# Mixture of experts: tokens gathered for two experts at a time, and the branch for crowded experts ahead of them

## The chip, the core and the metric

The kernel runs on one core of one Trainium2 chip. The metric is the device time of one execution in microseconds (us). PE is the matmul engine, ACT, DVE and POOL are the scalar, vector and general engines, SP issues the transfers.

## The reference

Four layers over 256 tokens of width 1024: two of a first kind (attention, feed-forward, a gated side input) and two of a second kind. Layer 1 of the first kind has a mixture of experts in place of its feed-forward, and there the change lies:

```python
def moe_swiglu(x, w_router, w_gate, w_up, w_down):      # x: 256 x 1024
    logits = (x @ w_router).astype(jnp.float32)         # 8 experts
    top_v, top_i = lax.top_k(logits, TOP_K)             # TOP_K = 2
    top_w = jax.nn.softmax(top_v, axis=-1)
    gates = jnp.sum(jax.nn.one_hot(top_i, N_EXPERTS) * top_w[..., None], axis=-2)
    out = jnp.zeros_like(x)
    for e in range(N_EXPERTS):                          # w_gate[e], w_up[e]: 1024 x 3584, w_down[e]: 3584 x 1024
        out = out + gates[..., e:e + 1] * swiglu(x, w_gate[e], w_up[e], w_down[e])
    return out
```

All is float32. The weights of the eight experts are 352 MB, which is 672 tiles of 128 x 1024 (512 KB each), 84 for each expert. The 256 tokens make 512 places with the experts, 64 for each on average.

## The kernel before

Nothing is issued where it is written. The builder's calls are recorded by `Plan` as operations; a list scheduler (`order`, `choose`, run in several passes over modelled costs, `simulate` and `backwards`) then writes out one order for each engine, and all recorded operations are issued from line L755 (copies on ACT from L753). Transfers all go through SP's queue, in the planned order, and cost what `RATE` (bytes per us) says. `keep_fast` puts dummy matmuls (bf16 `identb`, 128 x 512) into stretches where the model sees PE idle, to keep its clock up. Tiles of on-chip memory are slots of tags (mx 15, raw 5, w4 8, v4 4, kv 2); a transfer into a slot can start when the slot's last reader is done. In the expert stage `raw_moe` gives the order in which weight tiles take tags: a string of 30 places.

The stage (`moe`): `route` turns the router's logits into ranks, the place of every token with its expert (`pos`), the counts per expert (`count`), the largest of them (`most`) and the gates (`gg`). Then for each expert: `gather_whole` makes one-hot matrices of `pos` and multiplies the tokens `xs` (a high and a low part, fp32r) by them, 32 matmuls of 128 columns for up to 128 places. The hidden width 3584 goes in four chunks (1024, 1024, 1024, 512). For each, `expert_up` does gate and up, `expert_out` the chunk's part of down; that makes twelve calls of `tiled` per expert. Weights are the moving side of these matmuls and tokens the stationary side: for the first 64 places each tile takes two matmuls of 64 x 512 (`x2` in an order, four records in a trace). Behind that come two guarded blocks, one if the expert has over 64 tokens and one if over 96, each with 32 places and four matmuls of 32 x 256 per tile. A guarded block is a real branch on PE against a register with the expert's count (the registers are read on L750, the branches are L732). Products of gate and up are transposed on PE (28 blocks per expert), and `combine` scatters an expert's output back to the tokens with its one-hots.

In the middle of expert 4, behind its first chunk, stands `overflow_experts`: a branch of all engines on `most` (read on L1617, branch and its end on L294). If an expert has over 128 tokens, a loop goes through all weights for the tokens beyond 128. On this input it is jumped over. At this branch an engine has finished what stands ahead of it, and SP waits until its transfers have landed.

The guarded blocks, as they are recorded:

```python
for q in range(2):
    with nc.group((count, 64 + 32 * q, 0.5 - 0.5 * q)):   # the last number: share of the cost that the planner takes
```

Of the kernel before, what the change touches and what calls it, by code (L numbers as in the profile page):

```python
# [130 lines left out]
class Op:  # L131
    __slots__ = ("idx", "engines", "calls", "cost", "preds", "succs", "need", "tiles", "cp", "end", "eng", "done",
                 "table", "bytes", "start", "seq", "pri", "late", "after", "port", "columns", "when")
# [100 lines left out]
class Plan:  # L234
# [61 lines left out]
    def add(self, engines, method, args, kw):  # L296
# [13 lines left out]
        if engines == (DMA,):  # L310
            v = out if isinstance(out, View) else args[1]
            op.bytes += v.arr.size * SIZE[v.dtype]
        for e in op.cost:
# [58 lines left out]
    def paths(self, ops):  # L372

        for op in reversed(ops):
# [4 lines left out]
            op.cp += min(op.cost.values()) if e != DMA else 1.1 + op.bytes / self.RATE  # L379

    def order(self, ops, state, aside):
# [72 lines left out]
        out = []  # L454
        for _ in range(len(ops)):
# [17 lines left out]
            if e == DMA:  # L473
                op.start = max(op.start, state["dma"] - 6.0)
                go = max(state["dma"], op.start + 1.1)
                state["dma"] = op.end = go + op.bytes / self.RATE
# [181 lines left out]
    def backwards(self, segments, orders):  # L658
# [17 lines left out]
        for op in sorted(flat, key=lambda o: -o.end):  # L676
# [6 lines left out]
            if op.eng == DMA:  # L683
                run = op.bytes / self.RATE
# [55 lines left out]
    RATE = 370e3  # L740
# [42 lines left out]
class Net:  # L783
    def __init__(self, ctx, tc, a, out):
# [4 lines left out]
        self.raw_moe = ([("mx", 15), ("raw", RAW), ("mx", 15), ("w4", 8)] * RAW  # L789
                        + [("mx", 15), ("v4", 4), ("mx", 15), ("kv", 2)] * 2 + [("mx", 15), ("w4", 8)])  # L790
# [565 lines left out]
    def route(self, lg):  # L1356

        nc = self.nc
        rank = self.sm([128, 2, 8], "rank")
# [29 lines left out]
        nc.vector.tensor_copy(self.count, pt)  # L1389
        s1 = self.sm([128, 2, 8], "s1")  # L1390
# [18 lines left out]
        gg = self.one([128, 2, 8, 2], "gg", F32R)  # L1409
        nc.vector.tensor_copy(gg[:, :, :, 0], s1)  # L1410
        nc.vector.tensor_tensor(out=gg[:, :, :, 1], in0=s1, in1=gg[:, :, :, 0].bitcast(F32), op=OP.subtract)
        return gg, pos
# [7 lines left out]
    def gather_whole(self, e, xs, pos):  # L1420

        nc = self.nc
        P = self.one_hots(e, pos)
        xg = self.t4([128, KT, 128], "xe")
        for k0 in (0, 4):
            ps = self.pc([128, 4, 128], "gth")
            with nc.group():
                for k in range(4):
# [3 lines left out]
            self.copy_out(xg[:, k0:k0 + 4], ps)  # L1432
        return xg, P
# [5 lines left out]
    def weights(self, w, r0, nk, c0, n):  # L1439

        raw = self.nc.tile([128, nk, n], F32, "raw", *self.next_raw())
        self.nc.sync.dma_start(raw, w[r0:r0 + 128 * nk, c0:c0 + n].rearrange("(t p) c -> p t c", p=128))
        return raw

    def tiled(self, acc, slots, units, count, first, last):
# [19 lines left out]
    def up_weights(self, w, c0, n, k0=0):  # L1465
        nk = 1024 // n
        return [self.weights(w, 128 * k, nk, c0, n) for k in range(k0, KT, nk)]

    def expert_up(self, xg, count, wg, wu, c0, n):
# [3 lines left out]
        for w in (wg, wu):  # L1473
            acc = [self.pb([128, 512], "gu") for _ in range(2)]
            nc.vector.memset(acc[1], 0.0)
            self.tiled(acc, lambda k, s, m: xg[:, k, s:s + m], self.up_weights(w, c0, n), count, True, True)
            ps.append(acc)
        hT = self.ta([128, 2, n // 256, 128], "hT")
        for p in range(2):
            s = self.t2([128, n // 2], "sg")  # L1480
            nc.scalar.activation(s, ps[0][p][:, :n // 2], AF.Silu)
            nc.vector.tensor_tensor(out=s, in0=s, in1=ps[1][p][:, :n // 2], op=OP.mult)
            tp = self.pc([128, n // 256, 128], "hT")
# [661 lines left out]
```

## Time and profile before

| | us |
|---|---|
| median of 3 runs | 2297.81 |
| lowest, highest | 2297.07, 2299.12 |
| the profiled execution | 2294.73 |
| its span on the chip | 2293.0 |
| PE busy | 2160.0 (94%) |
| DVE busy | 1015.0 (44%) |
| ACT busy | 771.1 (34%) |
| POOL busy | 195.4 (9%) |

Read the page from its busy shares to the 40 slices, each of 57 us, then to the rows of single stretches. The expert stage is the one with few PE weight loads (PEld at 3 and 4 tenths) and a high DMA rate, from about 475 to 1495 us. A releaser is what ended an engine's idle time; PEq is PE's own sequencer, which runs its branches. Matmuls overlap their neighbours, so the distance of two starts is what one costs, and its length is more.

### The profile page before, as it was taken

The page shows a single profiled execution, that of the slowest core. Times are in us where ns is not written, and L with a number is a line of the kernel's source. Part 1 is how long each engine was busy: PE and PEld are TensorE (multiplying, and loading weights), DVE is VectorE, ACT ScalarE, POOL GpSimd, SP SyncE. Part 2 cuts the span into 40 slices and gives each one's busy share as a digit, 9 for nine tenths or more (in the row PEclk, how much of TensorE's full clock was granted, in tenths as well). Part 3 has the DMA queues.
Part 4 walks back from the last instruction along what each step waited for, and adds up shares of the span by engine and source line. Part 5 has one row for each costly group of instructions (what it writes and reads, how often), then busy time and mean ns, then how long its engine had stood idle before and what let it go on. Part 6 is the DMA issues. An engine that isn't in the chain of part 4 may idle for free. (4 is left out here: it accounts for less than half of the span.)

```text
span 2293.0 us, 36297 instructions
## 1 busy us (share of the span) xinstructions
PE 2160.0 (94%) x14885; PEld 1498.2 (65%) x14885; DVE 1015.0 (44%) x1678; ACT 771.1 (34%) x1156; POOL 195.4 (9%) x126
## 2 busy tenths in 40 slices
PE   8999998989899899988889999989999999999998
PEld 6899996863334343433333343459979998888997
DVE  6754567641011111111110201187677767867766
ACT  5444444511011110010010101057365556646554
POOL 0210001020000000000000000024220003611000
PEclk9999999979999999999999999999999999999999
DMA  7355654279978999899999899754355655425563
GB/s 244 119 185 184 191 186 138 74 281 403 375 294 332 408 354 383 289 361 354 379 351 380 334 330 390 258 158 130 105 182 166 193 177 151 139 85 182 180 193 120
DMA packets 246523, 558.27 MB, mean 243 GB/s; under 512 B 21320, under 2 KB 108552, under 8 KB 246280
## 3 DMA queue, kind: packets, MB, share of 16 engines
q1 hardware_dynamic: 246280, 554.72, 68.4%
q8 instruction: 190, 3.11, 0.5%
q14 instruction: 53, 0.43, 0.1%
HBM read 553.60 MB, written 1.05 MB: 242 GB/s over the span
## 5 line engine op out<-in xcount | busy, mean ns | idle before, releaser
L755 DVE TENSOR_TENSOR lo<-raw,hi 128x1024 fp32r<-128x1024 f32 x329 | 408.3, 1257 | 197.2 <-PE B L755 59.0
L755 ACT ACTIVATE hi<-raw 128x1024 fp32r<-128x1024 f32 x364 | 380.3, 1061 | 303.9 <-PE A L755 112.4
L755 PE MATMUL B<-r,hi 128*128 128x256 f32 x2112 | 386.6, 283 | 0.0
L755 PEld LDWEIGHTS B<-r,hi 128*128 128x128 f32 x2112 | 338.8, 191 | 12.8
L755 PE MATMUL A<-hi,r 128*128 128x512 f32 x896 | 332.0, 409 | 1.6 <-DVE v L755 1.1
L755 PE MATMUL B<-mx,w 128*64 128x512 f32 (+3 forms) x2048 | 309.1, 454 | 23.2 <-PEq L732 21.8
L755 PE MATMUL B<-r,lo 128*128 128x256 f32 x1056 | 298.8, 283 | 0.0
L755 PEld LDWEIGHTS B<-mx,w 128*64 128x64 f32 (+1 forms) x2048 | 114.0, 125 | 162.2 <-issue 122.3
L755 ACT ACTIVATE w<-B 128x512 f32<-128x512 f32 (+2 forms) x95 | 51.2, 541 | 501.4 <-PEq L732 286.3
L755 PE MATMUL B<-w,w 128*128 128x128 f32 (+4 forms) x1388 | 195.8, 378 | 11.1 <-PEq L732 7.4
L755 PEld LDWEIGHTS B<-r,lo 128*128 128x128 f32 x1056 | 202.0, 191 | 0.0
L755 PEld LDWEIGHTS A<-hi,r 128*128 128x128 f32 x896 | 170.7, 191 | 34.9 <-DVE v L755 1.7
L755 DVE MEMSET B<- 128x512 f32 x64 | 31.0, 485 | 365.7 <-ACT w L755 355.9
L755 PE MATMUL C<-hi,r 128*128 128x512 f32 x512 | 184.6, 399 | 4.8 <-DVE r L755 4.3
L755 PE MATMUL A<-lo,r 128*128 128x512 f32 x448 | 177.3, 396 | 0.6 <-DVE lo L755 0.6
L755 DVE TENSOR_TENSOR w<-w,B 128x512 f32<-128x512 f32 (+1 forms) x79 | 49.4, 625 | 277.9 <-PEq L732 178.2
L755 PE MATMUL A<-mx,v 128*64 128x512 f32 (+1 forms) x896 | 153.9, 492 | 7.7 <-PEq L732 5.9
L755 PEld LDWEIGHTS B<-w,w 128*128 128x128 f32 (+2 forms) x1388 | 110.2, 151 | 71.9 <-issue 50.7
L755 POOL TENSOR_TENSOR lo<-raw,hi 128x1024 fp32r<-128x1024 f32 x35 | 88.0, 2525 | 472.7 <-ACT hi L755 371.7
L753 ACT ACTIVATE v<-C 128x512 f32<-128x512 f32 (+1 forms) x49 | 25.9, 528 | 264.9 <-PE C L755 197.7
L755 PEld LDWEIGHTS C<-hi,r 128*128 128x128 f32 x512 | 97.8, 191 | 24.4 <-DVE r L755 5.2
L755 PE MATMUL C<-lo,r 128*128 128x512 f32 x256 | 101.5, 397 | 0.0
(235 smaller groups left out, 2704.0 us busy)
## 6 DMA issues: line engine op xcount, KB each, us to landing
mx<-in_w_exp_gate_dram SPq DMA_DIRECT2D x112, 512.0 KB
mx<-in_w_exp_up_dram SPq DMA_DIRECT2D x112, 512.0 KB
mx<-in_w_exp_down_dram SPq DMA_DIRECT2D x112, 512.0 KB
raw<-in_ffn_up_dram SPq DMA_DIRECT2D x88, 512.0 KB
raw<-in_w_in_dram SPq DMA_DIRECT2D x56, 512.0 KB
w<-in_w_exp_down_dram SPq DMA_DIRECT2D x46, 512.0 KB
w<-in_w_exp_gate_dram SPq DMA_DIRECT2D x45, 512.0 KB
raw<-in_ffn_down_dram SPq DMA_DIRECT2D x44, 512.0 KB
```

The costliest lines, as they stand in the source:

```text
L753: eng.activation(args[0], args[1], AF.Copy)
L755: getattr(eng, method)(*args, **kw)
```

## The change

- `gather_pair` gathers for two experts at once, 32 matmuls of 256 columns per pair, where `gather_whole` did 32 of 128 for each. One-hots are made again for each expert's `combine`.
- An expert's special path has 96 places instead of 128: one guarded block (over 64 tokens) per call of `tiled` instead of two, 96 in all instead of 192. The second accumulators are 256 wide instead of 512, an expert transposes 21 blocks instead of 28, and `slot_rows` copies three pieces per half and clears the last 32 rows on POOL.
- `overflow_experts` is taken where an expert has over 96 tokens and covers 96 to 352 in two passes of pairs. It stands right behind the routing and the split of the tokens. Its own weights go through v4 slots.
- `fetch` records the first 22 weight loads (raw, kv and mx slots) ahead of `route`, so ahead of that branch. `raw_moe` becomes a string of 28.
- `route` is split: the gates (`gates`) are worked out behind the branch, and once more within it.
- The planner takes 400e3 instead of 370e3 bytes per us for transfers whose rows have 1024 elements or more.

```diff
-    RATE = 370e3
+    RATE = {False: 370e3, True: 400e3}
...
-        self.raw_moe = ([("mx", 15), ("raw", RAW), ("mx", 15), ("w4", 8)] * RAW
-                        + [("mx", 15), ("v4", 4), ("mx", 15), ("kv", 2)] * 2 + [("mx", 15), ("w4", 8)])
+        self.raw_first = [("raw", RAW)] * RAW + [("kv", 2)] * 2 + [("mx", 15)] * 15
+        size = {"m": ("mx", 15), "r": ("raw", RAW), "w": ("w4", 8), "v": ("v4", 4), "k": ("kv", 2)}
+        self.raw_moe = [size[c] for c in "mrmwmrmvmwmkmrmwmrmvmwmkmrmm"]
...
-    def gather_whole(self, e, xs, pos):
...
+    def gather_pair(self, e, xs, pos):
+
+        nc = self.nc
+        P = self.r2([128, 2, 256], "P")
+        for j in range(2):
+            for b in range(2):
+                nc.vector.tensor_scalar(P[:, b, 128 * j:128 * j + 128], self.iota, pos[:, b, e + j:e + j + 1], None, op0=OP.is_equal)
+        xg = [self.t4([128, 4, 256], "xe") for _ in range(2)]
+        for k0 in range(0, KT, 2):
+            ps = self.pc([128, 2, 256], "gth")
             with nc.group():
-                for k in range(4):
+                for k in range(2):
                     ks = slice((k0 + k) * 128, (k0 + k) * 128 + 128)
                     for i in range(4):
                         nc.tensor.matmul(ps[:, k, :], lhsT=xs[i // 2][i % 2][:, ks], rhs=P[:, i // 2, :], start=i == 0, stop=i == 3)
-            self.copy_out(xg[:, k0:k0 + 4], ps)
-        return xg, P
+            self.copy_out(xg[k0 // 4][:, k0 % 4:k0 % 4 + 2], ps)
+        return xg
...
+    def weights(self, name, e, r0, nk, c0, n):
+
+        raw = self.fetched.pop((name, e, r0, c0), None)
+        if raw is None:
...
+    def fetch(self):
+
+        self.raw_tags = self.raw_first
+        for name, c0, n in (("gate", 0, 8), ("up", 0, 8), ("gate", 1024, 6)):
+            for k in range(n):
+                key = "w_exp_" + name, 0, 128 * k, c0
+                self.raws = len(self.fetched) - 1
+                self.fetched[key] = self.weights(*key[:3], 1, c0, 1024)
...
-        for q in range(2):
-            with nc.group((count, 64 + 32 * q, 0.5 - 0.5 * q)):
-                for k, u in enumerate(tiles):
-                    for i in range(4):
-                        mm(acc[1][32 * i:32 * i + 32, q * n // 4:(q + 1) * n // 4], lhsT=slots(k, 64 + 32 * q, 32),
-                           rhs=u[:, i * n // 4:(i + 1) * n // 4], start=whole and k == 0, stop=whole and k == k1 - 1)
...
+        with nc.group((count, 64, 1.0)):
+            for k, u in enumerate(tiles):
+                for i in range(4):
+                    mm(acc[1][32 * i:32 * i + 32, :n // 4], lhsT=slots(k, 64, 32), rhs=u[:, i * n // 4:(i + 1) * n // 4],
+                       start=whole and k == 0, stop=whole and k == k1 - 1)
...
+            self.nc.gpsimd.memset(z[h][96:128, :], 0.0)
             self.copy_out(z[h][0:64, :], y[0][64 * h:64 * h + 64, :])
-            for q in range(2):
-                for i in range(2):
-                    self.copy_out(z[h][64 + 32 * q:96 + 32 * q, 256 * i:256 * i + 256],
-                                  y[1][64 * h + 32 * i:64 * h + 32 * i + 32, 256 * q:256 * q + 256])
+            for i in range(2):
+                self.copy_out(z[h][64:96, 256 * i:256 * i + 256], y[1][64 * h + 32 * i:64 * h + 32 * i + 32, :])
...
     def moe(self, logits):
         nc, a, tc = self.nc, self.a, self.tc
-        gg, pos = self.route(logits)
+        self.fetch()
+        rank, pos = self.route(logits)
...
+        self.overflow_experts(logits, rank, xs, pos)
+        gg = self.gates(logits, rank, "gg")
...
-                if c == 0 and e == N_EXP // 2:
-                    self.expert_out(y, prev, count, wd[e], 0, widths[0], True, False)
-                    prev = None
-                    tags, self.raw_tags = self.raw_tags, [("raw", RAW)]
-                    self.overflow_experts(xs, pos, gg)
-                    self.raw_tags = tags
...
-        nc.enter(lambda: tc.If(self.real.values_load(most[0:1, 0:1].ap(), min_val=0, max_val=S) > 128))
+        nc.enter(lambda: tc.If(self.real.values_load(most[0:1, 0:1].ap(), min_val=0, max_val=S) > 96))
...
+        for skip in (96, 224):
+            nc.vector.tensor_scalar(beyond, pos, -float(skip), None, op0=OP.add)
+            for e in range(0, N_EXP, 2):
```

The order of PE at the end of a call of `tiled` in expert 0, before (B are accumulators, w and mx weight tiles or gathered tokens by slot; the tokens are the second name of `32x256` rows):

```order
L755 MATMUL B_136<-w_161,w_166 32x256 x4
L755 MATMUL B_136<-mx_2_3979,w_166 32x256 x4
L732 UNCONDITIONAL_BRANCH x2
L755 MATMUL B_138<-w_163,w_166 64x512 x2
L732 COMPARE_AND_BRANCH
L755 MATMUL B_137<-raw_148,w_166 32x256 x4
L755 MATMUL B_137<-mx_2_3987,w_166 32x256 x4
```

One block ends, one tile later the next one begins. The same place after:

```order
L756 MATMUL B_136<-mx_2_3989,w_164 32x256 x4
L733 UNCONDITIONAL_BRANCH x2
L756 MATMUL B_139<-mx_2_3998,w_164 64x512 x2
L756 MATMUL B_136<-mx_2_3991,w_162 64x512 x2
L756 MATMUL B_136<-mx_2_3999,w_162 64x512 x2
L756 MATMUL C_157<-ident_91,w_86 128x128 x4
L756 MATMUL B_136<-mx_2_3994,w_162 64x512 x2
L756 MATMUL B_136<-mx_2_4000,w_162 64x512 x2
L733 COMPARE_AND_BRANCH
L756 MATMUL B_137<-mx_2_3986,w_162 32x256 x4
```

One block ends, and what begins seven rows later is the block of the next call. All lines stand one further on in the changed file (L756 for L755, L733 for L732).

The order of PE where it comes to the branch over `most`, before, in expert 4 (r are scattered rows of `combine`):

```order
L755 MATMUL C_157<-r_167,r_187 128x512
L755 MATMUL C_157<-r_168,r_187 128x512
L755 MATMUL C_158<-r_167,r_187 128x512
L755 MATMUL C_158<-r_168,r_187 128x512
L1617 TENSOR_LOAD most_182
L294 COMPARE_AND_BRANCH
```

Ahead of it stands the end of expert 3's output. After, behind the routing:

```order
L756 LDWEIGHTS identb_92
L756 MATMUL A_147<-identb_92 128x512
L1634 TENSOR_LOAD most_188
L294 COMPARE_AND_BRANCH
L756 MATMUL C_157<-r_169,xs_2_3985 128x256
L756 MATMUL C_157<-r_169,xs_2_3982 128x256
```

Ahead of it stand dummy matmuls, behind it (in the branch's body, and again behind its end) the first gather. The order of SP there, before:

```order
L755 DMA mx_2_3980<-in_w_exp_up_dram 128x1024
L755 DMA v_143<-in_w_exp_up_dram 128x1024
L755 DMA mx_2_3982<-in_w_exp_up_dram 128x1024
L755 DMA kv_145<-in_w_exp_up_dram 128x1024
L294 COMPARE_AND_BRANCH x2
L294 UNCONDITIONAL_BRANCH x2
```

SP has issued tiles of expert 4 and waits at the branch. After:

```order
L756 DMA mx_2_3994<-in_w_exp_gate_dram 128x1024
L756 DMA mx_2_4000<-in_w_exp_gate_dram 128x1024
L756 DMA mx_2_3992<-in_w_exp_gate_dram 128x1024
L756 DMA mx_2_3997<-in_w_exp_gate_dram 128x1024
L1634 TENSOR_LOAD most_188
L294 COMPARE_AND_BRANCH x2
```

The last of the 22 loads of `fetch` stand ahead of the branch, all other weight loads behind its end. Elsewhere the planner's order changes in many places of the program; in the expert stage it places 144 dummy matmuls before and none after, in the rest of the program about as many as before.

## Rows read from the trace of the kernel before

**Rows 1.** Page, parts 1, 2: busy time; DMA share of 40 slices in tenths.

```profile
PE 2160.0 (94%) x14885; PEld 1498.2 (65%) x14885; DVE 1015.0 (44%) x1678; ACT 771.1 (34%) x1156; POOL 195.4 (9%) x126
...
DMA  7355654279978999899999899754355655425563
```

**Rows 2.** PE's timeline, stage's start: start and length (us), operation, [idle before, releaser].

```profile
498.06 7.06 PE L755 MATMUL C<-r,xs 128*128 128x128 f32 x32 [4.20 <-issue]
505.05 1.98 PE L755 MATMUL B<-w,w 128*64 128x512 f32 x4
```

**Rows 3.** Windows: us, busy time and count per engine, PE clock, DMA share, GB/s.

```profile
475.00:500.00 25.00, 18.68 (x78) 14.05 (x79) 15.36 (x53) 4.49 (x7) 11.28 (x6) 0.56 0.99 383
500.00:525.00 25.00, 22.70 (x94) 11.11 (x95) 2.35 (x4) 4.09 (x6) 0.00 (x0) 0.83 1.03 408
...
675.00:700.00 25.00, 24.82 (x192) 10.10 (x192) 5.61 (x9) 2.02 (x4) 0.00 (x0) 1.00 0.54 194
...
1025.00:1050.00 25.00, 16.25 (x59) 5.17 (x60) 2.12 (x8) 0.60 (x1) 0.00 (x0) 0.82 0.95 357
```

**Rows 4.** PE's timeline, tiles of a light expert, then of a heavy one.

```profile
551.55 1.06 PE L755 MATMUL A<-mx,v 128*64 128x512 f32 x4
552.41 1.06 PE L755 MATMUL B<-mx,w 128*64 128x512 f32 x4
553.61 1.08 PE L755 MATMUL B<-kv,w 128*64 128x512 f32 x4
554.84 1.08 PE L755 MATMUL B<-mx,w 128*64 128x512 f32 x4
...
614.64 0.64 PE L755 MATMUL B<-raw,w 128*32 128x256 f32 x8
...
617.69 0.61 PE L755 MATMUL B<-mx,w 128*32 128x256 f32 x8
```

**Rows 5.** PE's timeline behind the branch in mid-stage.

```profile
1028.40 1.97 PE L755 MATMUL B<-kv,w 128*64 128x512 f32 x4 [6.42 <-DVEq L294]
1030.13 1.95 PE L755 MATMUL B<-mx,w 128*64 128x512 f32 x4
```

**Rows 6.** Instructions of L732 (guarded blocks): count, ns min/median/max, first and last start.

```profile
L732 PEldq COMPARE_BRANCH  x240: 70/212/5062, 504.5 to 1488.5; - x120
L732 PEldq EVENT_SEMAPHORE  x144: 51/51/51, 507.1 to 1489.8; - x144
```

**Rows 7.** PE's waits in 475:1495: total us, times, longest.

```profile
PE B L755 <- PEq L732: 38.7, 55, 5.4
PE A L755 <- PEq L732: 11.9, 24, 2.1
```

**Rows 8.** PE by form in 475:1495: count, busy us, mean ns, idle before, releaser.

```profile
L755 PE MATMUL C<-ident,w 128*128 128x128 f32 x224 | 40.6, 289 | 2.0 <-PEq L732 1.3 <-ACT v L753 0.5 <-DVE w L755 0.2
...
L755 PE MATMUL C<-r,xs 128*128 128x128 f32 x256 | 34.9, 294 | 5.6 <-issue 4.2 <-ACT v L753 1.4
...
L755 PE MATMUL C<-identb 128*128 128x512 bf16 x117 | 29.7, 405 | 0.0
...
L755 PE MATMUL B<-identb 128*128 128x512 bf16 x27 | 7.1, 389 | 0.0
```

**Rows 9.** PE's timeline in a later stage, matmuls of 256 columns.

```profile
1730.75 0.40 PE L755 MATMUL B<-hi,r 128*128 128x256 f32 x2
1730.99 0.28 PE L755 MATMUL B<-lo,r 128*128 128x256 f32 x1
```

**Rows 10.** Windows around the branch in mid-stage.

```profile
1014.00:1016.00 2.00, 1.85 (x10) 0.57 (x8) 0.00 (x0) 0.00 (x0) 0.00 (x0) 1.00 0.15 61
1016.00:1018.00 2.00, 2.00 (x13) 0.73 (x10) 0.00 (x0) 0.00 (x0) 0.00 (x0) 1.00 0.37 37
```

**Rows 11.** PE's instructions of L294 (the branch), then L750 (counts).

```profile
L294 PEldq COMPARE_BRANCH  x1: 6276/6276/6276, 1021.7 to 1021.7; - x1
...
L750 PEldq TENSOR_LOAD <-count x8: 300/306/499, 494.3 to 503.8; - x8
```

More of the change, by code (lines that the diff above doesn't have):

```diff
@@ L132 @@
     __slots__ = ("idx", "engines", "calls", "cost", "preds", "succs", "need", "tiles", "cp", "end", "eng", "done",
-                 "table", "bytes", "start", "seq", "pri", "late", "after", "port", "columns", "when")
+                 "table", "bytes", "start", "seq", "pri", "late", "after", "port", "columns", "when", "rate")
 def columns_of(method, args, kw):
@@ L378, in paths @@
                 op.cp = max(op.cp, s.cp + self.lat(e, s.engines[0]))
-            op.cp += min(op.cost.values()) if e != DMA else 1.1 + op.bytes / self.RATE
+            op.cp += min(op.cost.values()) if e != DMA else 1.1 + op.bytes / op.rate
     def order(self, ops, state, aside):
@@ L475, in order @@
                 go = max(state["dma"], op.start + 1.1)
-                state["dma"] = op.end = go + op.bytes / self.RATE
+                state["dma"] = op.end = go + op.bytes / op.rate
                 free[e] = op.start + 0.1
@@ L683, in backwards @@
             if op.eng == DMA:
-                run = op.bytes / self.RATE
+                run = op.bytes / op.rate
                 tail = max(tail, busy[DMA])
@@ L1469, in expert_up @@
-    def expert_up(self, xg, count, wg, wu, c0, n):
+        with nc.group((count, 64, 1.0)):
[3 more added lines that the diff above has]
+                       start=whole and k == 0, stop=whole and k == k1 - 1)
+    def expert_up(self, e, xg, count, c0, n):
         nc = self.nc
         ps = []
[L1473 to L1476, printed above, removed]
-            ps.append(acc)
[L1478 to L1483, printed above, removed]
-            for f in range(n // 256):
+        nk = 1024 // n
+        for w in ("w_exp_gate", "w_exp_up"):
+            acc = [self.pb([128, 512], "gu"), self.pb([128, 256], "gu")]
+            nc.vector.memset(acc[1][:, :n // 4], 0.0)
+            units = [self.weights(w, e, 128 * k, nk, c0, n) for k in range(0, KT, nk)]
+            j = 128 * (e % 2)
+            self.tiled(acc, lambda k, s, m: xg[k // 4][:, k % 4, j + s:j + s + m], units, count, True, True)
+            ps.append(acc)
+        hT = self.ta([128, 6, 128], "hT")
+        for p, (i, f1) in enumerate(((0, n // 256), (4, n // 512))):
+            s = self.t2([128, 128 * f1], "sg")
+            nc.scalar.activation(s, ps[0][p][:, :128 * f1], AF.Silu)
+            nc.vector.tensor_tensor(out=s, in0=s, in1=ps[1][p][:, :128 * f1], op=OP.mult)
+            tp = self.pc([128, f1, 128], "hT")
+            for f in range(f1):
@@ L1485, in expert_up, with expert_out @@
                 nc.tensor.transpose(tp[:, f, :], s[:, f * 128:f * 128 + 128], self.ident)
-            self.copy_out(hT[:, p], tp)
+            self.copy_out(hT[:, i:i + f1], tp)
         return hT
-    def expert_out(self, y, hT, count, wd, c0, n, first, last):
-        units = [self.weights(wd, c0 + 128 * k, 1, 0, D) for k in range(n // 128)]
+    def expert_out(self, e, y, hT, count, c0, n, first, last):
+        units = [self.weights("w_exp_down", e, c0 + 128 * k, 1, 0, D) for k in range(n // 128)]
@@ L1495, in slots @@
                 i, f = divmod(k, n // 256)
-                return hT[:, 0, f, 64 * i:64 * i + 64]
+                return hT[:, f, 64 * i:64 * i + 64]
             i, f = divmod(k, n // 512)
-            return hT[:, 1, (s - 64) // 32 * (n // 512) + f, 32 * i:32 * i + 32]
+            return hT[:, 4 + f, 32 * i:32 * i + 32]
         self.tiled(y, slots, units, count, first, last)
     def zero(self, acc, start):
-        self.nc.tensor.matmul(acc, lhsT=self.causb[:, 0, :], rhs=self.nc.filler[1], start=start, stop=not start)
+        self.nc.tensor.matmul(acc, lhsT=self.causb[:, 0, :], rhs=self.nc.filler[1][:, :2, :], start=start, stop=not start)
     def slot_rows(self, y):
@@ L1528, in any_chunk @@
                     k = 2 * g + t
-                    mm(acc, lhsT=xg[:, k, :], rhs=raw[:, t, :], start=k == 0, stop=k == KT - 1)
+                    mm(acc, lhsT=xg[k // 4][:, k % 4, j:j + 128], rhs=raw[:, t, :], start=k == 0, stop=k == KT - 1)
             ps.append(acc)
@@ L1539, in any_chunk @@
         for f in range(4):
[L1540 removed]
+            raw = nc.tile([128, 1, D], F32, "raw", "v4", 4)
             nc.sync.dma_start(raw, lambda f=f: wd[bass.ds((c0 + 128 * f).value(), 128), :].rearrange("(t p) c -> p t c", p=128))
```

74 lines of the change are left out of this document (35 added, 39 removed).

## The prediction

> **What bounds the kernel now.** I read the page from the top: PE is busy for 94% of the span [rows 1], so the first question is where PE has work that is no work. The DMA line of the same group shows where loads could matter: the expert stage (slices 9 to 26) moves 300 to 400 GB/s, the rest half of that. The stage starts its loads at 475 us (0.99 in 475:500 [rows 3]), does its first weight matmul at 505.05 [rows 2] and has its last guarded block at 1490 [rows 6]. Its windows say what rules inside it [rows 3]: in 500:525 the loads run flat out (share 1.03, 408 GB/s, so a 512 KB weight tile takes 524,288 / 408,000 = 1.285 us), in 675:700 they idle for half the time (0.54) while PE is full. Bare tile work says why. A tile costs PE 0.86 us for the first 64 slots (551.55 to 552.41; at half clock 1.73, from 1028.40 to 1030.13) and 0.43 us more where an expert has over 64 tokens (eight tiles from 614.64 to 617.69 and one step more) [rows 4, 5]. So a light expert of 84 tiles takes 72 us of tile work against 108 us of loads, a heavy one 108 against 108 with its transposes, gathers and output on top. Which are which: of 240 branch tests and jumps at the guarded blocks, 144 ended in a skip [rows 6], so 192 blocks, 48 of them run, which is four experts of twelve calls. The router on the reference's inputs gives 57, 71, 63, 69, 64, 55, 66 and 67 tokens: 1, 3, 6 and 7 are heavy, and nobody is over 96. PE bounds the heavy experts; in the light ones PE and the loads are nearly level, and the slots (28 after, one or two more before) carry some 36 us of lead from one to the next. The last view was the list of PE's waits: the guarded blocks alone hold 38.7 and 11.9 us of it [rows 7].
>
> **The change, part by part** (minus is a gain).
>
> *Guarded blocks, 192 to 96.* The second of each pair, never run here, goes. Its waits: (38.7 + 11.9) / 192 = 0.26 us each [rows 7], so 96 x 0.26 = -25 us. Start to start it is more: 553.61 - 552.41 - 0.86 = 0.34 us, and 0.37 at the next [rows 4], or -34. From below: where PE would wait for a weight anyway the branch is free, as in half the experts: -13. I take -25, the measured waits. The dearest branch took 5.1 us with a median of 0.21 [rows 6], so a few long ones carry much of the sum, and it is chance which of them go.
>
> *Fillers.* In before the planner puts 144 dummy matmuls into the expert stage to keep the clock up, in after none: 29.7 + 7.1 = 37 us of busy time [rows 8]. Where they stood in a wait they cost nothing, so 0 to -37; the waits for loads in the light half would have been there, so I take half, -18.
>
> *Gathers.* 256 matmuls of 128 columns hold PE for 34.9 us [rows 8]; 32 of them ran at half clock in 7.06 [rows 2], so the rest took 27.8 / 224 = 0.124 each. The pairs need 128 of 256 columns. Before has that width in another stage, two in 0.24 us [rows 9], 0.12 each: the width is free. First pair at half clock 32 x 0.24 = 7.7, the other 96 x 0.12 = 11.5, together 19.2: -16, and 0 in experts where PE waits for loads. I take -14, since the rows of busy time overlap a little with their neighbours.
>
> *Transposes.* 28 to 21 per expert, 56 fewer: 40.6 / 224 = 0.18 us each [rows 8], -10. The copies that follow them get narrower on ACT and DVE, which are under half busy; nothing.
>
> *The branch in mid-stage.* PE stood 6.42 us at it and then ran four tiles at 1.73 instead of 0.86 us [rows 5]: -6.4 - 3.5 = -10. SP waited there for all its loads to land, and the DMA engines had shares of 0.15 and 0.37 for 4 us [rows 10], 3 us of loads lost. Both now fall at the stage's start.
>
> *The start.* In before PE stood 4.20 us ahead of the first gather, gathered for 7 us and met its first weight at 505.05 [rows 2], with some 23 tiles landed. Now PE's queue holds the eight count reads (0.31 us each [rows 11]), some 15 fillers, the read of `most` and the branch, which took PE 6.28 us in mid-stage [rows 11], and only then the gather of 128 x 256 columns at half clock, 7.7 us. The count reads were there before too. So the first weight comes later by the jump and some change: 5 to 12 us, I take +7. Queued behind PE's branch is everything that it does for the experts; behind SP's the loads from the 23rd on. SP issues 22, waits until all have landed (about 505), and can then fill eight slots more; for the next PE must free one, which it does after some 13 tiles, about 527. So the loads rest for 3 us at the branch and about 11 behind those eight. PE starts with 30 tiles in hand, 39 us of loads, so it doesn't notice in the first expert; the loads do, if they rule later. That is in the next term and its range.
>
> A sentence of the Trainium skill speaks against the change here. "Runtime: NRT & Kernel Launch", section "Instruction fetch mechanics", says that a taken branch whose target lies outside the instructions fetched so far has to fetch them before the engine goes on; the 6.28 us on PE [rows 11] agree. By it the jump is as dear at the stage's start as in its middle, whatever the length of the body; the sum has it on both sides already, so it stays as it is.
>
> *What the loads give back.* Added up, -25 - 18 - 14 - 10 - 10 + 7 = -70. But a light expert would then take PE about 85 us (72 tiles, 4 for twelve branches, 4 transposes, 2 gather, 3 output) against 108 us of loads, eating 23 us of lead, and a heavy one about 120, giving back 12. The lead of 36 us lasts for one light expert, not for experts 4 and 5 in a row. Ifs, gathers and transposes save 49 us, 24 of them in light experts; half of these I take as lost to waits: +12 (0 to +24). Sum: **-58 us**. Outside the stage the planner has reshuffled the order; PE is full there before and after, and I put that at 0, +-8.
>
> From the profiled execution, 2294.73 (span 2293.0 and 1.73 around it): 2236.7. The median of the runs is 3.1 higher, so **2240 us**.
>
> **Rivals.**
>
> *The loads become the bound.* For it: the sum of bare PE work, 4 x 85 + 4 x 120 = 820 us, is less than the 672 x 1.285 = 863 us that the loads need; and the rests at the start come on top. Against it: the share of 0.54 in a heavy expert [rows 3], where the loads have room that a PE 10 us faster takes from nobody. Then all 24 us in light experts go, the fillers were cover for waits (18 more), and the 11 us rest counts: -70 + 24 + 18 + 11 = -17, **2281 us**.
>
> *PE never waits.* For it: the loads run flat out in 500:525 with PE at 22.7 of 25 us beside them. Then all takes its upper end: -34 - 37 - 16 - 10 - 10 + 5 = -102, **2196 us**.
>
> *Slower: the clock falls in the light experts.* Fillers are gone there, and PE waits for loads. What a wait does is in [rows 5]: after the 6.42 us at the branch tiles took 1.73 us, the pace of the lower of the two levels (1.2 instead of 2.4 GHz), 0.87 more each. The gain of 58 is used up from 67 of the 336 light tiles on; at a third of them, 112 x 0.87 = +97, the time is **2337 us**. Against it: at half clock PE needs 1.73 a tile and the loads 1.285, so the lead grows, the waits stop and the clock comes back; it can't last through an expert. The Trainium skill, "TensorE: Matmul & The Clock Gate", section "HAM oscillation — how this bites in real kernels", describes just this: a kernel that waits for data between short bursts of matmuls is throttled again each time. In 1025:1050, behind the 6.42 us wait, the mean granted clock was 0.82 [rows 3], which agrees for a long wait; no row here shows what many short ones do.
>
> *It doesn't do what it says.* With an expert over 96 the general path would go twice through all weights, 2 x 863 us on top, near 4,000 us. The skip counts [rows 6] and the tokens speak against it: 1 in 200.
>
> **How the numbers follow.** Chances: the forecast (2215 to 2260) 0.52; loads as the bound (2260 to 2285) 0.22; PE never waits (2196 to 2215) 0.13; near no change 0.04; the clock 0.085; the general path 0.005. A measurement tells 0.2%, 4.6 us, from nothing. Faster 0.87, same 0.04, slower 0.09. The range for 8 in 10 leaves out the fastest end and all that is slower: **2200 to 2285**.
>
> **What would show it.** Right: one test and at most one skip per call at the guarded blocks, 96 in all, and their waits at some 25 us; no dummy matmul behind the first weight; DMA shares of 1.0 in the light experts and higher than 0.6 in the heavy ones; first weight matmul at 510 to 517; a light expert in 90 to 105 us, a heavy one in 120 to 128; clock 1.00 nearly everywhere. Wrong: weight loads at the head of PE's list of waits (the first rival), granted clocks under 0.9 in several light windows (the third), or any long stretch of loads from the branch's body (the fourth). If the waits at the guarded blocks hold as much as before, the long branches were not a matter of number, and my largest term falls.

## The result and the profile after

| | before | after |
|---|---|---|
| median, us (4 runs each) | 2298.47 | 2223.65 |
| lowest, highest | 2297.07, 2301.7 | 2218.64, 2227.26 |
| span of the profiled execution | 2293.0 | 2223.0 |
| first weight matmul | 505.05 | 509.65 |
| last weight tile of the stage | 1490.7 | 1419.0 |

The ratio is 0.9671, with a 95% interval from 0.9649 to 0.9693: 75 us less, where 58 were forecast and the range held. The span says where: 76.3 us between the first and the last weight tile, 4.6 given back at the start, 1.7 more behind the stage, so the shuffled order elsewhere did next to nothing.

The page after, parts 1 to 3 (busy time, the DMA share in slices, the queue that brings instructions: packets, MB, share), answers to [rows 1]:

```profile
PE 2102.1 (95%) x14582; PEld 1449.2 (65%) x14582; DVE 984.3 (44%) x1670; ACT 751.7 (34%) x1141; POOL 224.7 (10%) x147
...
DMA  7356664349999999999999998544455664435563
...
q8 instruction: 141, 2.31, 0.4%
```

Slices 10 to 24 are now full of loads almost without a break. The kernel before had 190 packets of instructions where this one has 141, a row to remember below. PE's waits in the expert stage after (total us, times, longest), against [rows 7]:

```profile
PE B L756 <- DMA v<-in_w_exp_gate_dram: 34.9, 4, 11.1
PE B L756 <- DMA mx<-in_w_exp_up_dram: 8.4, 6, 4.9
PE A L756 <- issue: 6.3, 1, 6.3
PE C L756 <- PEq L733: 3.6, 15, 0.4
...
PE B L756 <- PEq L733: 2.9, 16, 0.4
...
PE A L756 <- PEq L733: 1.7, 7, 0.4
```

The list has turned over. The guarded blocks (now L733) hold 8.2 us instead of 52.1, and weight loads lead with some 49 us (all rows of loads), where before they held about 13. The blocks' instructions, against [rows 6]:

```profile
L733 PEldq COMPARE_BRANCH  x144: 65/176/632, 519.6 to 1416.2; - x144
L733 PEldq EVENT_SEMAPHORE  x48: 51/51/51, 524.1 to 1199.9; - x48
```

Half as many blocks, as forecast, but the longest branch went from 5062 to 632 ns: not half of the long ones are gone, nearly all are. Over 0.45 us took 30 of 240 branches before, and take 2 of 144 now. Four windows of the stage after (us, busy time and count for each engine, PE clock, DMA share, GB/s), against [rows 3]:

```profile
500.00:525.00 25.00, 21.55 (x107) 9.53 (x107) 6.84 (x33) 2.95 (x5) 1.13 (x2) 0.97 0.77 286
...
575.00:600.00 25.00, 15.90 (x104) 7.35 (x100) 1.15 (x4) 1.53 (x4) 0.52 (x1) 0.87 1.03 403
...
675.00:700.00 25.00, 25.00 (x260) 10.75 (x258) 1.44 (x4) 2.56 (x5) 0.00 (x0) 1.00 0.87 322
...
1150.00:1175.00 25.00, 14.37 (x62) 5.58 (x60) 1.30 (x4) 0.60 (x1) 0.52 (x1) 0.73 1.03 409
```

In a heavy expert (675:700) PE is full and the loads nearly. In light ones (575:600, 1150:1175) the loads run flat out and PE stands. The wait at the end of the first light expert, in PE's timeline (start, length, operation, idle before and releaser):

```profile
602.65 1.97 PE L756 MATMUL B<-v,w 128*64 128x512 f32 x4 [11.12 <-DMA v<-in_w_exp_gate_dram]
604.38 1.95 PE L756 MATMUL B<-mx,w 128*64 128x512 f32 x4
606.09 1.54 PE L756 MATMUL A<-mx,v 128*64 128x512 f32 x4
```

It waits 11 us for one load, then runs its next tiles at 1.7 us, half clock (a granted clock of 0.54 from 602.6 to 607.5), and is back at 0.86 after three or four. Every light expert ends so.

For each expert, the time from its first weight tile to the next expert's first (us; L light, H heavy; the last three columns are experiments told below). It is counted in PE's 2944 matmul rows of the first 64 places, 368 for each expert. At the borders the planner mixes tiles of two experts, and not alike before and after, so a row is good to some 3 us between those two; kernels with the same order compare more closely.

| expert | before | after | before, one block | after, short second block | after, half loads |
|---|---|---|---|---|---|
| 0 L | 105.2 | 103.0 | 100.2 | 103.6 | 82.9 |
| 1 H | 125.0 | 121.1 | 120.7 | 125.5 | 121.1 |
| 2 L | 115.7 | 103.6 | 107.2 | 104.0 | 91.7 |
| 3 H | 131.7 | 121.5 | 126.8 | 125.4 | 121.4 |
| 4 L | 125.4 | 103.7 | 114.8 | 103.6 | 91.9 |
| 5 L | 119.9 | 113.7 | 108.7 | 113.2 | 91.9 |
| 6 H | 130.2 | 115.6 | 125.3 | 119.5 | 115.6 |
| 7 H | 132.6 | 127.2 | 127.7 | 131.8 | 127.2 |

### The profile page after: what moved, and what is told of

The parts are those of the page before. It is cut to its first block, busy times and chain, and to the rows that moved or that the text cites. A ratio compares the mean times of both kernels' runs of the same rounds, so it can differ in the third digit from the quotient of the medians.

```text
span 2223.0 us, 35510 instructions
## 1 busy us (share of the span) xinstructions
PE 2102.1 (95%) x14582; PEld 1449.2 (65%) x14582; DVE 984.3 (44%) x1670; ACT 751.7 (34%) x1141; POOL 224.7 (10%) x147
## 5 line engine op out<-in xcount | busy, mean ns | idle before, releaser
L756 DVE TENSOR_TENSOR lo<-raw,hi 128x1024 fp32r<-128x1024 f32 x324 | 404.7, 1257 | 200.3 <-PE B L756 94.6
L756 ACT ACTIVATE hi<-raw 128x1024 fp32r<-128x1024 f32 x364 | 382.2, 1062 | 292.8 <-PE B L756 123.5
L756 PE MATMUL B<-r,hi 128*128 128x256 f32 x2112 | 388.2, 282 | 0.0
L756 PEld LDWEIGHTS B<-r,hi 128*128 128x128 f32 x2112 | 342.0, 191 | 17.7
L756 PE MATMUL B<-mx,w 128*64 128x512 f32 (+3 forms) x2188 | 327.9, 458 | 10.6 <-DMA mx<-in_w_exp_up_dram 8.4
L756 PE MATMUL A<-hi,r 128*128 128x512 f32 x896 | 334.3, 410 | 0.9 <-DVE v L756 0.6
L756 PE MATMUL B<-r,lo 128*128 128x256 f32 x1056 | 298.6, 283 | 0.0
L756 PEld LDWEIGHTS B<-mx,w 128*32 128x32 f32 (+1 forms) x2188 | 111.0, 124 | 153.1 <-issue 104.3
L756 PEld LDWEIGHTS B<-r,lo 128*128 128x128 f32 x1056 | 201.5, 191 | 0.0
L756 PEld LDWEIGHTS A<-hi,r 128*128 128x128 f32 x896 | 171.1, 191 | 32.2 <-DVE v L756 1.4
L756 PE MATMUL C<-hi,r 128*128 128x512 f32 x512 | 185.1, 400 | 1.1 <-ACT kv L756 1.1
L756 DVE MEMSET B<- 128x256 f32 (+1 forms) x64 | 15.7, 245 | 370.0 <-ACT w L756 366.6
L756 PE MATMUL A<-lo,r 128*128 128x512 f32 x448 | 177.4, 396 | 0.2 <-DVE lo L756 0.2
L756 PE MATMUL B<-w,w 128*128 128x128 f32 (+4 forms) x1252 | 168.4, 363 | 0.3 <-PEq L733 0.3
L756 PE MATMUL A<-mx,v 128*32 128x256 f32 (+1 forms) x960 | 162.1, 491 | 0.2 <-PEq L733 0.2
L754 ACT ACTIVATE v<-C 128x512 f32<-128x512 f32 (+2 forms) x63 | 29.4, 467 | 379.8 <-PE C L756 336.0
L756 DVE TENSOR_TENSOR w<-w,B 128x256 f32<-128x256 f32 (+2 forms) x79 | 41.8, 529 | 247.9 <-PE B L756 229.7
L756 POOL TENSOR_TENSOR lo<-raw,hi 128x1024 fp32r<-128x1024 f32 x40 | 102.0, 2563 | 487.8 <-ACT hi L756 367.4
L756 PEld LDWEIGHTS B<-w,w 128*128 128x128 f32 (+2 forms) x1252 | 104.5, 155 | 51.4 <-issue 39.6
L756 ACT ACTIVATE w<-B 128x256 f32<-128x256 f32 (+3 forms) x95 | 44.7, 475 | 264.8 <-PE B L756 242.9
L756 PEld LDWEIGHTS C<-hi,r 128*128 128x128 f32 x512 | 98.5, 192 | 18.8 <-ACT kv L756 1.9
L756 PE MATMUL B<-raw,w 128*64 128x512 f32 (+3 forms) x648 | 100.9, 463 | 1.3 <-DMA raw<-in_w_exp_up_dram 1.0
## 6 DMA issues: line engine op xcount, KB each, us to landing
mx<-in_w_exp_down_dram SPq DMA_DIRECT2D x120, 512.0 KB, 10.3
```

What stands on the lines that cost most here:

```text
L754: eng.activation(args[0], args[1], AF.Copy)
L756: getattr(eng, method)(*args, **kw)
```

## The experiments

My theory after the result (A): the guarded block that never runs costs by the instructions that PE passes over, which still have to be fetched among the weight loads; and the changed stage is bound by PE in heavy experts and by the loads in light ones. The rivals: each branch has its price (B); the dummy matmuls were the gain; the move of the branch was.

### The second block taken out of the kernel before

```diff
+                    if op.when and op.when[1] == 96:
+                        continue
                     if op.when:
```

> The kernel before without its second guarded blocks (over 96 tokens, never run on this input; left out, the order of all else unchanged). In the kernel before the blocks held 52 us of PE's waits and 30 of 240 branches took over 0.45 us; after, 8 us and 2 of 144. Theory A, the long branches come from two blocks that are jumped one close behind the other: they go altogether, waits at blocks fall to about 10 us, and with some of it given back to waits for loads the time is 2255 to 2270. Rival B, each jump has its own chance of being long: about half remain (some 15 over 0.45 us, waits of 25 us), 2272 to 2280.

Measured: 2238.58 us against 2298.86, ratio 0.9743 (0.9712 to 0.9774): 60 us from one deletion, more than either theory had. Its blocks' branches (count, ns min/median/max):

```profile
L734 PEldq COMPARE_BRANCH  x144: 65/174/4028, 501.6 to 1431.5; - x144
```

Its instruction queue on the page:

```profile
q8 instruction: 143, 2.34, 0.4%
```

Three of 144 branches took over 0.45 us, against 30 of 240; packets fell from 190 to 143, as in the kernel after. The largest row of waits at the blocks is 5.6 us where [rows 7] has 38.7. So for the branches theory A holds as it was expected here, two blocks close one behind the other, and four fifths of the whole change is this. By the table 35 us fell away in the light experts, where both blocks were passed over and 21 of the 30 long branches lay, and 19 in the heavy ones, 0.40 for each of 48 branches. The time fell by more than PE's waits at the blocks, which went from 52.1 to 7.0. One reason is that the list of waits holds only part of what a branch costs (next experiment). Another may lie in SP's list of waits: a slot comes free for the next load only when the block that reads it is passed, so SP stood behind the blocks as well. No run took the two apart. In the kernel before this row led the list (total us, times, longest):

```profile
SPq L755 <- PEq L732: 178.1, 37, 16.2
```

In the kernel after the blocks come ninth, with 27.3 us in 13 waits.

### A second block put into the kernel after: full, short, and inside the first

One PE operation behind each block a second one that never runs, with the same 32 matmuls or with one:

```diff
+                        again = op
                         continue
...
+                    if again and op.eng == PE:
+                        with self.tc.If(again.when[0].value() > 96):
+                            for method, args, kw in again.calls:      # short: again.calls[:1]
+                                self.call(again, method, args, kw)
```

> The kernel after with a second guarded block (over 96 tokens, never run, same 32 matmuls) one PE operation behind each first one, order of all else unchanged. Theory A, two blocks jumped in close succession make the long branches: they come back (20 or more over 0.45 us, waits of 30 to 50 us), partly hidden where PE waits for loads: 2240 to 2265. Rival B, each jump costs the same as now: 8 us of waits become 16, 2228 to 2234.

> As the one with two blocks, but the second block holds a single matmul, so as many branches and hardly any instructions to jump over. If the instructions jumped over make the long branches: none come back, some 0.1 to 0.15 us for each of the 93 branches, 2228 to 2238. If the number of branches makes them: as with the full second block.

Measured: full 2275.26 us (ratio 0.9905, 0.9873 to 0.9936), so 52 us of the gain are gone again; short 2242.11 (0.9747, 0.9717 to 0.9778). The new branches (L742) of the full one:

```profile
L742 PEldq COMPARE_BRANCH  x93: 202/325/5607, 521.0 to 1461.2; - x93
```

Its instruction queue has 187 packets, that of the short one 144. The same branches of the short one:

```profile
L742 PEldq COMPARE_BRANCH  x93: 202/208/342, 523.7 to 1432.8; - x93
```

With equally many branches, none of the new ones is long where there is nothing to pass over, and 21 are over 0.45 us where there are 32 matmuls. Among the first blocks 11 more are long with the full second block, 6 with the short one. The short one costs 18 us. By the table 17 of them lie in the heavy experts, 0.35 for each of their 48 branches, and none in the light ones, which wait for loads anyway. That is a branch's own price, and PE's listed waits at the blocks show only 4.3 us of it (8.2 to 12.5). The other 33 us of the full block are the length. Whether two branches in succession are needed:

```diff
                             for method, args, kw in op.calls:
                                 self.call(op, method, args, kw)
+                            with self.tc.If(op.when[0].value() > 96):
+                                for method, args, kw in op.calls:
+                                    self.call(op, method, args, kw)
```

> The kernel after with the never-run second block put inside the first one: 96 jumps at the outer branch as now, but in the four light experts each passes over 64 matmuls instead of 32; the heavy ones pass over the inner 32. Theory A, it is the length of the instructions passed over that stalls a branch: long branches (over 0.45 us) come back in the light experts, 10 to 20 of them, and the time is 2235 to 2260. Rival B, two branches in succession are needed: none come back, 2222 to 2232.

Measured: 2275.32 us (0.9915, 0.9889 to 0.9941), dearer than both theories and the same as two blocks. The outer branch, and who waited for it (us, times):

```profile
L733 PEldq COMPARE_BRANCH  x96: 70/160/6157, 515.1 to 1459.7; - x96
...
  PE A L759: 19.3, 9
...
  PE B L759: 10.3, 16
```

In the light experts PE comes to no second branch, and yet 32 of the outer branches are over 0.45 us, 29 of them in light experts, and the instruction queue is back at 188 packets. So how long a branch takes is decided by the length of what it passes over. The time is another matter: counted as in the table, the light experts grew by only 9 us, since they wait for loads anyway, and the heavy ones by 44. There PE runs the outer block and then passes over the inner 32 matmuls, with 5 inner branches over 0.45 us; why that costs 0.9 us a call, where the short block cost 0.35, is open.

That a long branch is a wait for instructions I read from the kernel before at its second longest branch, 5.05 us from 766.8. These are the queues from 766 to 773 us (packets, MB, share of 16 engines): the weight loads fill the engines, and one packet of instructions passes between them, at 769.3 to 770.4; the branch ends 1.4 us later.

```profile
q1 hardware_dynamic: 780, 2.82, 101.2%
q8 instruction: 1, 0.02, 1.0%
```

The packets' times in the trace show the same for nearly all: 29 of the 30 long branches end 1.33 to 1.54 us after a packet of instructions has come in, and of the 210 short ones only 4 end 1.25 to 1.65 us after one. In the runs with two blocks and with the nested block all 32 and all 37 long branches do, and so does PE's branch over `most`, before and after (1.4 us behind a packet). The Trainium skill, "Runtime: NRT & Kernel Launch", section "Instruction fetch mechanics", says that a branch to a target not yet fetched waits for its page; these branches agree.

The count of packets says something else, how long the code is. The passed-over code is fetched with the rest: the 47 packets that left with the 96 second blocks are 8 KB a block. Counted with all passed-over blocks, PE's matmuls and weight loads come to 66 bytes each in the kernels before, after and with one block; without them it would be 105, 79 and 79. No run shows where the limit in length lies: 32 matmuls passed over alone were almost free, 64 in a row or nearly in a row were not.

### The dummy matmuls taken out of the kernel before

```diff
+        orders = [[o for o in order if o.idx >= 0 or not lo <= o.start <= hi] for order in orders]
```

(lo and hi are the planned times of the expert stage's first and last PE operation.)

> The kernel before without the dummy matmuls of its expert stage (129 in the trace, 28 to 37 us of PE), order of all else unchanged. Theory A, half of them stood in PE's way: 2280 (2275 to 2288). Rival B, they all stood in PE's way: 2262 to 2270. Rival C, they stood in waits for loads or kept the clock up: 2298 or more, with lower granted clocks in 1000:1200.

Measured: 2295.26 us against 2298.86, ratio 0.9991 (0.9973 to 1.0009). No difference. 144 matmuls of PE are gone, 37 us of rows in [rows 8], and waits took the place of about half of them: PE's busy time in 475:1495 fell from 927.1 to 907.5 us, in a stage as long as before. These are the waits:

```profile
PE B L758 <- PEq L735: 37.3, 56, 5.3
...
PE B L758 <- DMA v<-in_w_exp_gate_dram: 9.0, 2, 5.6
PE A L758 <- DMA w<-in_w_exp_down_dram: 8.2, 3, 7.9
```

The blocks wait as long as in [rows 7], the first row of loads was 2.3 us before. So what the dummies filled was time in which PE stood or would have stood. The mean granted clock of 475:1495 fell from 0.97 to 0.95, as rival C had it, and that cost nothing measurable.

### The branch for crowded experts: left out, and back in the middle

```diff
+            if aside or step and step.__name__ != "switch":
+                continue
```

The first kernel leaves the branch and the general path out where the planned order is written out (a crowded expert would not be computed), with the order of the rest kept. The second calls it where it stood before, behind expert 4's first chunk:

```diff
-        self.overflow_experts(logits, rank, xs, pos)
...
+                if c == 0 and e == N_EXP // 2:
+                    self.expert_out(e, y, prev, count, 0, widths[0], True, False)
+                    prev = None
+                    self.overflow_experts(gg, xs, pos)
```

> The kernel after without the branch for crowded experts (left out, so experts over 96 tokens would not be computed), order of all else unchanged. Its price at the stage's start: PE's jump of 6 us and the rest of the loads (shares of 0.90 and 0.77 in the first 50 us, some 8 us of loads). Theory A, the loads bound the light experts, so their rest counts: 2209 to 2218. Rival B, both are hidden behind the first expert's lead: 2219 to 2225.

> The kernel after with the branch for crowded experts back in the middle of expert 4, all else of the change kept; the planner orders it anew. If the move itself gains what the prediction said (10 us saved in mid-stage, 7 given at the start): 2224 to 2230. If the rest of loads at the start cost as much as the stop in mid-stage: 2215 to 2224. If mid-stage is dearer, since light experts 4 and 5 wait for loads there: 2230 to 2245.

Measured: without it 2219.06 us (0.9660, 0.9639 to 0.9681), in the middle 2218.10 (0.9658, 0.9634 to 0.9683). Against 0.9671 (0.9649 to 0.9693) neither is told from the kernel after; the move is worth nothing, and by the ratios costs some 3 us, within the noise. The first kernel is no clean price of the jump. The 15 dummy matmuls that stood beside the branch stay in PE's order ahead of the first gather, so the first weight tile comes no sooner than the 509.65 of the kernel after:

```profile
500.20 6.15 PE L758 MATMUL A<-identb 128*128 128x512 bf16 x15 [6.35 <-issue]
...
509.23 2.80 PE L758 MATMUL B<-raw,w 128*64 128x512 f32 x12
```

The second kernel shows both places. Its first weight tile comes 12.9 us sooner, 4.0 of them because the planner's other order ends the routing sooner (its last matmul at 487.38 instead of 491.38). In the middle its wait is 6.6 us:

```profile
496.71 1.08 PE L756 MATMUL B<-raw,w 128*64 128x512 f32 x4
...
PE B L756 <- DMA v<-in_w_exp_gate_dram: 26.3, 4, 8.9
PE B L756 <- DVEq L294: 6.6, 1, 6.6
```

Counted as in the table, its expert 4 takes 114.2 us, 10.5 more than in the kernel after, and expert 5 takes 111.6, 2.1 less; the waits for that load are 26.3 instead of 34.9. So the stop in mid-stage costs some 8 us and the start of the kernel after some 13; the whole runs differ by 5.5 us at most, which the noise doesn't tell from nothing.

### Half of every load

```diff
...
+        elif place:                       # not the first load into this slot
+            n = args[0].shape[-1] // 2
+            args = [v[:, :, :n] for v in args]
...
```

The other half of a tile keeps old data, so only times count here. Done to both kernels.

> The kernel after with each expert's weight loads cut to half their columns behind the first load into a slot (the other half of a tile keeps old data, so the result is not the reference's), the issue order unchanged. PE's work is the same. Theory A, PE waits 49 us for loads in the light experts and loses some more at half clock behind these waits: 2160 to 2180. Rival B, the waits come from the order of slots and not from the rate: 2205 to 2224.

> The kernel before with each expert's weight loads cut to half their columns behind the first load into a slot (the result is not the reference's), issue order unchanged. The same cut took 67 us off the kernel after. Theory A, before was bound by PE and its branches, so the loads held little, 15 to 30 us: 2265 to 2283, and the change gave the difference, 35 to 50 us, back to the loads. Rival B, the loads held as much before: 2225 to 2240. Rival C, lighter load traffic also shortens the long branches (their waits fall well under 52 us): then the time falls by that much more, and the page of waits tells it from B.

Measured: after 2156.78 us, 67 less than the kernel after (65 by the ratios); before 2261.58, 34 less than its comparison of 2295.84. In the table above all light experts of the kernel after fall by 12 to 22 us and no heavy one moves by more than 0.1: the loads held some 66 us, all in light experts. The window at the end of the first one, against the 15.90 us and 0.87 above:

```profile
575.00:600.00 25.00, 24.69 (x178) 11.05 (x176) 1.42 (x5) 1.53 (x4) 0.52 (x1) 1.00 0.51 174
```

In the kernel before, some of the 34 us are not loads:

```profile
PE B L762 <- PEq L733: 24.2, 52, 3.1
PE A L762 <- PEq L733: 8.2, 24, 0.9
```

Its waits at the blocks fell from 52.1 to 33.9 us (1.5 of it in a third row) and its branches over 0.45 us from 30 to 14, with equally many packets of instructions (190): with less traffic the instructions come sooner, which is expectation C beside A. With light loads the change would have been worth 2261.6 - 2156.8 = 105 us; some 30 of them go back to the loads.

### Seven loads earlier, and the gathers twice

```diff
+            self.fetch(0, 7)
             nc.layout(1)
             self.moe(logits)              # now fetches loads 7 to 21
```

> The kernel after with 7 of the 22 first weight loads (five raw and two kv slots) recorded ahead of the change of layout, in a stretch where the loads rest (shares of 0.08 and 0.00 in 425:475); PE's order is the same to the row. Theory A, the loads bound the light experts: 7 tiles of 1.285 us, so 5 to 9 us less, 2215 to 2219. Rival B, PE or the branch at the start bounds: no change, 2221 to 2226.

> The same 7 early loads in the kernel with the branch in the middle of expert 4 (2218 us). Theory A: 2209 to 2214. Rival B: 2216 to 2220.

Measured: 2219.51 us (0.9657, 0.9643 to 0.9670) and, with the branch in the middle, 2218.49 (0.9658, 0.9644 to 0.9672). At most 4 us for 9 us of loads. The windows of the first show why:

```profile
450.00:475.00 25.00, 24.08 (x140) 20.59 (x139) 17.11 (x36) 7.00 (x15) 2.39 (x1) 1.00 0.34 103
...
500.00:525.00 25.00, 23.44 (x120) 10.30 (x120) 7.75 (x35) 3.34 (x6) 1.24 (x2) 1.00 0.57 204
```

The loads do run earlier (0.34 where the kernels before and after had none), and rest the longer behind the branch (0.57 instead of 0.77), since all slots are full until PE frees some. The first expert ended 4.5 us sooner, and all later ones kept their length.

```diff
-                    for i in range(4):
+                    for i in [0, 1, 2, 3] * 2:
```

> The kernel after with the four matmuls of each gathered block done twice (128 more matmuls of 256 columns, about what the pairs saved): 128 x 0.12 = 15 us of PE more. If PE's removed work counts in full: 2238 to 2240. If what falls into light experts and the start is hidden behind the loads, as theory A has it: 2225 to 2233.

Measured: 2239.58 us (0.9744, 0.9729 to 0.9759), 16 more: every microsecond counted. Its gathers by form (count, busy us, mean ns, idle before):

```profile
L756 PE MATMUL C<-r,xs 128*128 128x256 f32 x256 | 33.9, 286 | 1.7 <-DVE r L756 1.7
```

Those of the kernel after, against 34.9 us in [rows 8]:

```profile
L756 PE MATMUL C<-r,xs 128*128 128x256 f32 x128 | 19.4, 293 | 3.3 <-DVE sm L756 3.2
```

Theory A had wanted part of it hidden. But the pairs are gathered at the start and at the ends of experts 1, 3 and 5; experts 1 and 3 are heavy and grew by 4 and 5 us, and the start by 4. Only in expert 5, which is light, did theory A have a claim, and there it failed: 3.4 us more, with the wait at its end as long as before (10.3 us). Why that wait did not shrink is open.

## Why the prediction held, and which steps did not

The range held the time, and the sign of the largest term was right. That the sum came within 17 us is in part luck: single terms were off by 15 to 35 us, and these errors partly met.

*Guarded blocks, -25.* The step that failed in size: it is -60 alone. I divided the waits of [rows 7] by the number of branches and took half. [rows 6] had it that a few long ones carry the sum, and I called it chance which would go. It was not: long ones need a long way to jump, and with one block of each pair gone nearly all went. PE's waits at the blocks fell by 44 us, 52.1 to 8.2, instead of 25. And the waits were too small a measure: the 0.34 us from start to start in [rows 4], which I set aside, is what a branch cost in the heavy experts (0.35 and 0.40), where nothing else hides it.

*Fillers, -18.* Failed: -2, with an interval from -6 to +2. They stood in waits. The bound of 0 was the right one, for the reason that I gave for halving it.

*Gathers, -14.* Right in size: the rows say 34.9 to 19.4, and the width is nearly free; doubling them cost 16.

*Transposes, -10.* Too large by the rows: 40.6 us of [rows 8] became 35.4 for 168, so 56 fewer gave about 5. Why each holds more, 0.21 instead of 0.18, is open, and no run took them apart from the rest.

*The branch, -10 in mid-stage and +7 at the start.* PE's jump took 6.06 us at the start, and the first weight matmul came at 509.65, 4.6 later than in [rows 2]:

```profile
497.86 5.09 PE L756 MATMUL A<-identb 128*128 128x512 bf16 x15 [6.31 <-issue]
506.13 3.59 PE L756 MATMUL C<-r,xs 128*128 128x256 f32 x24 [3.19 <-DVE sm L756]
509.65 2.79 PE L756 MATMUL B<-raw,w 128*64 128x512 f32 x12
```

The gather itself ran at full clock (granted 1.00 in 506:510), behind dummies, in 0.15 us a matmul: I had put it at half. What holds it back is that DVE, too, stands until PE's jump has ended, and makes the one-hots only then:

```profile
504.65 1.41 DVE L756 TENSOR_SCALAR r<-iota,pos 128x128 fp32r<-128x128 f32 x4 [12.57 <-PEq L294]
```

The -10 in mid-stage was about right: with the branch back in the middle experts 4 and 5 take 8.4 us more. The +7 was too small. Against the kernel before the start is only 4.6 later, but against the same kernel with the branch in the middle it is 12.9, 9 of them between the routing and the first tile. So the move is worth nothing, where I had it at -3.

*The loads, +12.* The mechanism was right and the size too small: some 30 us against light loads, and waits for loads of 49 instead of 13 us. I let half of what light experts save be lost. Between the kernel before with one block and the kernel after, the heavy experts save 15 us and the light ones 7, no more than the 8 of the branch that left their middle; so nearly all of what gathers and transposes save in light experts is lost there. A light expert takes 103 to 114 us with its loads and 83 to 92 with half of them. The second blocks are the exception: their 35 us in light experts were gained, since the long branches made those longer than their loads. The new string of slots, the planner's new rate and the split routing were never tried alone.

*Rivals.* The loads as the bound came true in half of the stage, and the sign that I named for it, loads at the head of PE's waits, is there: they need 863 us in a stage that has 909 from its first weight tile to its last. It was no reason against a gain, since in heavy experts the loads do have room. "PE never waits" had the fillers and the blocks as its prices; of these only the blocks were real. The slower rival was there in small: the granted clock fell to 0.73 in 1150:1175, and three tiles or so behind each long wait ran at half clock. As the prediction had it, it ended itself, for at 1.7 us a tile PE takes longer than a load does (1.285), and the loads get ahead again.

## What to carry to other kernels

Code that a branch passes over isn't free: it is fetched with the rest, and where the transfers are full its fetch waits in line. Look at the spread of a branch's length, not at its mean, and at what comes in just before a long one ends; the count of the instruction queue's packets tells only how long the code is. And before pricing PE work that is saved, ask for each part of a stage which resource ends last there: here a branch cost 0.35 us in a heavy expert, and nothing in a light one.

## What the runs showed of the hardware

- A long branch ends when code has come in: of those over 0.45 us in the kernel before, 29 of 30 end 1.33 to 1.54 us after a packet of the instruction queue, of the short ones 4 of 210.
- Passing over 32 matmuls (a block of one `tiled` call) took at most 0.63 us in the kernel after, and in the kernel before with one block three times more, up to 4.03. In all runs with one block, 1 to 6 branches were over 0.45 us. With a second block behind the first or inside it (64 matmuls to pass over in light experts, 32 in heavy ones) 30 to 37 were, up to 6.16, with the full weight traffic.
- Code that is never run is fetched: 96 blocks of it were 47 packets of 16 KB.
- The same branches were shorter with half the weight traffic: 33.9 us of waits instead of 52.1, 14 long ones instead of 30.
- A branch with almost nothing to pass over cost 0.35 us in heavy experts, where PE is full, and nothing in light ones, where it waits for loads.
- A gather matmul of 256 columns held PE hardly longer than one of 128: 19.4 / 128 = 0.15 us against 34.9 / 256 = 0.14.
